# Low parts of weight tiles: a negated copy by ScalarE and an adding DMA in place of a subtraction by POOL

## The chip, the core and the metric

The kernel runs on one core of a Trainium2 chip. The core has five instruction streams that work side by side and wait for one another through semaphores: TensorE (PE, matrix products), VectorE (DVE), ScalarE (ACT), GpSimd (POOL) and SyncE (SP, which here only issues DMAs). Sixteen DMA engines move data between HBM and the on-chip memory (SBUF). Each stream is worked through strictly in the order in which it was written.

The metric is the time of one execution on the device, in microseconds (us); lower is better.

## The reference

One layer of a bidirectional hybrid encoder, in float32, for 1024 tokens of width 1024:

```python
h = _rms_norm(x, g_mix_pre[l])
proj = h @ w_in[l]
...
attn_o = _window_attention(aq, ak, av, attn_sink[l])
dn_o = _gated_deltanet(dqkv, dgate, dalpha, dbeta, conv_w[l], a_log[l], dt_bias[l], g_dn_out[l])
mix = jnp.concatenate([attn_o, dn_o], axis=-1) @ w_out[l]
x = x + _rms_norm(mix, g_mix_post[l])
c = _memory_cross_attention(_rms_norm(x, g_cross_pre[l]), _rms_norm(mem, g_mem[l]), w_cq[l], w_ckv[l], w_co[l])
x = x + _rms_norm(c, g_cross_post[l])
f = _swiglu(_rms_norm(x, g_ffn_pre[l]), w_gate_up[l], w_down[l])
x = x + _rms_norm(f, g_ffn_post[l])
```

What matters here is that all weight matrices pass once through TensorE, and that the products must come out close to float32.

## The kernel before, in words

**High and low parts.** The kernel gives TensorE its operands in a rounded float32 type (fp32r). To keep the accuracy, each operand is split into a high part (the value rounded to fp32r) and a low part (value minus high part, again as fp32r), and a product is made of three: high by high, high by low, low by high. The helper `split(hi, lo, src, scale, eng)` makes the two parts: ScalarE copies `src` into `hi` (line 102), then VectorE or, with `eng=nc.gpsimd`, POOL subtracts (line 103). So every weight tile goes through a chain: DMA load from HBM, ScalarE cast, subtraction, matmuls.

**Weight tiles.** `load_w` (lines 119 to 130) loads a tile of 128 partitions by 1024 floats (512 KB) into `wraw` (line 125) and splits it into `whi` and `wlo`. The pool `wp` has two buffers of each of the three. A new `wraw` can be loaded when the split of the tile two before has read the old one; a new `whi` or `wlo` can be written when the matmuls of the tile two before have read the old one. The loads stand in SP's one queue, between all other DMAs of the kernel, and are given a high priority so that they are placed early.

**Who asks POOL to subtract.** Five callers give `eng=nc.gpsimd`:

- `delta_proj`: 10 of the 12 projections of the DeltaNet part of `w_in`; two matmul halves for each tile (`gemm_b`, line 259).
- `next_keys`: 8 tiles of `w_ckv` (line 902, matmuls on line 906), one in each step of the delta-rule scan, between two window-attention blocks (`ORDER_3`). The scan's steps load `kv` and `pz` (lines 786 and 787) through the same SP queue.
- `cross_q`: 16 tiles of `w_cq` (line 1069), 24 matmuls each, in two rounds of 8; the second round's matmuls stand between those of the first half's cross attention.
- `pair_weights`: 14 tiles of `w_gate_up` for the 7 feed-forward blocks that weren't begun early (line 1240).
- Line 1150: 8 tiles of 128 by 512 of the normed activations (`xraw`), for the feed-forward part.

That makes 48 tiles of 128x1024 and 8 of 128x512. The other splits of weights (60 of 128x1024) are subtracted by VectorE.

**Order.** A scheduler places the instructions of all engines from a timing model of its own when the program is built, so a change in one helper also moves other instructions. `ORDER_1` to `ORDER_3` give the order of the larger steps. Stages, by the span's clock: DeltaNet projections until about 211 us, windows and inverses until about 423, the scan with `next_keys` until about 600, output projection until 689, `cross_q` and cross attention 689 to 803, its output projection and the norm until about 1000, the feed-forward part to the end.

Of the kernel before, what the change touches and what calls it, by code (L numbers as in the profile page):

```python
# [14 lines left out]
ALU = mybir.AluOpType  # L15
# [60 lines left out]
def tile_hybrid_block(  # L76
# [6 lines left out]
    nc = tc.nc  # L83
# [9 lines left out]
    def f32(ap):  # L93
        return ap.bitcast(F32)
# [4 lines left out]
    def split(hi, lo, src, scale=None, eng=None):  # L99

        if scale is None:
            nc.scalar.copy(hi, src)  # L102
            (eng or nc.vector).tensor_tensor(lo, src, f32(hi), ALU.subtract)  # L103
        else:
            nc.scalar.activation(hi, src, AF.Identity, scale=scale)
            nc.vector.scalar_tensor_tensor(lo, src, scale, f32(hi), ALU.mult, ALU.subtract)
# [11 lines left out]
    def load_w(src, k, n, eng=None, after=None):  # L118

        with tc.high_priority(AHEAD):  # L120
            raw = wp.tile([P, k, n], F32, tag="wraw", name="wraw")
            with ExitStack() as order_:
                if after:
                    order_.enter_context(tc.issue_after(after.ins))
                nc.sync.dma_start(raw, src.rearrange("(k p) n -> p k n", p=P))
            hi = wp.tile([P, k, n], F32R, tag="whi", name="whi")
            lo = wp.tile([P, k, n], F32R, tag="wlo", name="wlo")
            split(hi, lo, raw, eng=eng)
        return hi, lo
# [79 lines left out]
    for hf in range(2):  # L209
        hi = hx.tile([P, KT, HALF], F32R, name=f"hhi{hf}")  # L210
        lo = hx.tile([P, KT, HALF], F32R, name=f"hlo{hf}")
        for j in range(4):
            t = 4 * hf + j
            xt = xts[t] if t < 6 else t1.tile([P, D], F32, tag="xt", name="xt", bufs=6)
            if t >= 6:
                nc.sync.dma_start(xt, x[t * P:(t + 1) * P, :])
            junk = t1.tile([P, D], F32, tag="junk", name="junk", bufs=1)
            ss = t1.tile([P, 1], F32, tag="ss", name="ss", bufs=4)
            nc.scalar.activation(junk, xt, AF.Square, accum_out=ss)
            rs = t1.tile([P, 1], F32, tag="rs", name="rs", bufs=4)  # L220
            rstd_of(rs, ss, 1.0 / D, EPS)
            nc.vector.scalar_tensor_tensor(xt, xt, rs, gmix, ALU.mult, ALU.mult)
            for kq in range(2):
                pt = small()
                for k in range(4):
                    c = (4 * kq + k) * P
                    nc.tensor.transpose(pt[:, k * P:(k + 1) * P], xt[:, c:c + P], ident)
                o = slice(4 * kq, 4 * kq + 4), slice(j * P, (j + 1) * P)
                split(hi[:, o[0], o[1]], lo[:, o[0], o[1]], pt.rearrange("p (k t) -> p k t", k=4))
        hT.append((hi, lo))  # L230
        dump(f"hT{hf}", (hi, lo))
# [380 lines left out]
    def window(n, g):  # L612
# [41 lines left out]
        for j in range(nb):  # L654
            pp = pw.tile([P, 512], F32, tag="pw", name="ptw")
            for hh in range(4):
                nc.tensor.transpose(pp[:, hh * P:(hh + 1) * P], pr[hh][:, j * P:(j + 1) * P], ident)
            ph = tw.tile([P, 512], F32R, tag="ph", name="ph")
            pl = tw.tile([P, 512], F32R, tag="pl", name="pl")
            split(ph, pl, pp)  # L660
            for i, pe_ in enumerate((ph, pl)):
                nc.tensor.matmul(po.rearrange("p h t -> p (h t)"), vhl[:, k0 + j, g].rearrange("p r e -> p (r e)"), pe_,
                                 start=(j == 0 and i == 0), stop=(j == nb - 1 and i == 1))
# [846 lines left out]
```

## Time and profile before

| | us |
|---|---|
| median of 3 runs | 1585.95 |
| lowest and highest | 1582.44, 1587.69 |
| span of the profiled execution (first to last instruction) | 1584.2 |
| busy: ScalarE | 762.6 |
| busy: POOL | 498.5 |

The profiled execution has no time of its own beside its span; the median lies 1.75 us above that span.

How the rows are read. A group of instructions has its line, engine, operation, what it writes and reads (`wlo<-wraw,whi`), the shape, the count, then busy time and mean duration in ns, and after the bar the idle time of the engine just before them with what ended it. A row of the timeline has the start in us, the duration in us, the engine, the line and the operation; in square brackets stands the idle time before it. A row on a tile has the shortest, median and longest duration in ns and the first and last start. Matmuls are pipelined: a row's duration is longer than the distance to the next matmul.

### The profile page before, as it was taken

Reading aid. Unit: us, or ns where it says so; the run is one execution under the profiler, and the core shown is the slowest. Engines: PE = TensorE matmul, PEld = TensorE weight load, DVE = VectorE, ACT = ScalarE, POOL = GpSimd, SP = SyncE. Lnnn points to the kernel's source line nnn. Section 1 sums busy time; section 2 is a strip of 40 time slices with the busy share of each in tenths; the row PEclk is TensorE's granted clock in tenths of the full one; section 3 lists DMA queues with packets and bytes.
Section 4 is the critical chain, followed back from the end, with each engine's and each line's share of the span. In section 5 each row is a group of like instructions: output and inputs, shape, how many; then the busy total and the mean of one; then the engine's idle time right before and its main releaser. Section 6 shows DMA issues by size and latency. Waiting matters only on the chain. (4 is left out here: it accounts for less than half of the span.)

```text
span 1584.2 us, 21184 instructions
## 1 busy us (share of the span) xinstructions
PE 1507.2 (95%) x7514; PEld 1261.1 (80%) x7514; DVE 1058.9 (67%) x1616; ACT 762.6 (48%) x1523; POOL 498.5 (31%) x447
## 2 busy tenths in 40 slices
PE   6999889989899989999999999999999999999997
PEld 5877778878689967788888777788888888888786
DVE  6846887985688865544346449677768654596665
ACT  6566543238766785554335566323232332344532
POOL 2368644233134510243301140433434333100021
PEclk9999999989999999999999999999999999999999
DMA  6134148383998576454222254443335333853354
GB/s 207 41 114 130 44 152 228 113 206 104 305 288 277 185 248 204 147 193 151 67 80 81 79 192 139 131 156 120 124 109 166 100 100 101 296 201 113 107 171 161
DMA packets 252151, 242.97 MB, mean 153 GB/s; under 512 B 33528, under 2 KB 187021, under 8 KB 252045
## 3 DMA queue, kind: packets, MB, share of 16 engines
q1 hardware_dynamic: 252045, 241.62, 48.1%
q8 instruction: 59, 0.97, 0.3%
q14 instruction: 47, 0.39, 0.1%
HBM read 172.07 MB, written 66.88 MB: 151 GB/s over the span
## 5 line engine op out<-in xcount | busy, mean ns | idle before, releaser
L102 ACT CAST whi<-wraw 128x1024 fp32r<-128x1024 f32 x108 | 113.3, 1050 | 162.4 <-PE pmg L1006 34.8
L103 POOL TENSOR_TENSOR wlo<-wraw,whi 128x1024 fp32r<-128x1024 f32 x48 | 120.2, 2504 | 192.8 <-ACT whi L102 174.5
L259 PE MATMUL pg<-hlo,whi 128*128 128x512 f32 x352 | 140.3, 399 | 0.0
L259 PE MATMUL pg<-hhi,whi 128*128 128x512 f32 x352 | 140.2, 399 | 0.0
L259 PE MATMUL pg<-hhi,wlo 128*128 128x512 f32 x352 | 140.0, 398 | 0.0
L103 DVE TENSOR_TENSOR wlo<-wraw,whi 128x1024 fp32r<-128x1024 f32 x60 | 74.6, 1244 | 79.9 <-ACT whi L102 75.7
L1006 PE MATMUL pmg<-whi,b 128*128 128x512 f32 x384 | 118.4, 394 | 2.6 <-ACT whi L102 2.2
L1181 PE MATMUL pA<-s,whi 128*128 128x512 f32 x352 | 109.5, 392 | 1.4 <-ACT m L1198 1.4
L284 DVE SCALAR_TENSOR_TENSOR acc<-cp,cols,acc 128x1024 f32<-128x1024 f32 x48 | 73.9, 1540 | 19.5 <-ACT acc L282 18.9
L1006 PEld LDWEIGHTS pmg<-whi,b 128*128 128x128 f32 x384 | 71.2, 188 | 17.9 <-ACT whi L102 2.7
L1258 POOL TENSOR_TENSOR act<-act,up 128x512 f32<-128x512 f32 x33 | 50.1, 1518 | 89.6 <-DVE up L1257 53.1
L259 PEld LDWEIGHTS pg<-hhi,wlo 128*128 128x128 f32 x352 | 67.3, 191 | 13.2
L259 PEld LDWEIGHTS pg<-hhi,whi 128*128 128x128 f32 x352 | 67.2, 191 | 13.4 <-ACT hhi L102 0.3
L259 PEld LDWEIGHTS pg<-hlo,whi 128*128 128x128 f32 x352 | 67.4, 191 | 13.1
L1371 PE MATMUL pdX<-dhl,whi 128*128 128x512 f32 x264 | 76.1, 390 | 1.5 <-DVE zv L1426 0.7
L1181 PEld LDWEIGHTS pA<-s,whi 128*128 128x128 f32 x352 | 65.3, 188 | 15.2 <-ACT m L1198 2.0
L1401 POOL TENSOR_SCALAR frs<-sq 128x1 f32<-128x1 f32 x8 | 12.0, 1500 | 196.0 <-ACT jk L1390 195.0
L1006 PE MATMUL pmg<-wlo,b 128*128 128x512 f32 x192 | 71.4, 391 | 0.0
L1181 PE MATMUL pA<-s,wlo 128*128 128x512 f32 x176 | 68.7, 392 | 1.6 <-DVE wlo L103 1.6
L102 ACT CAST whi<-araw 128x1024 fp32r<-128x1024 f32 (+1 forms) x36 | 35.3, 982 | 70.8 <-PE pdX L1371 27.6
L1230 POOL TENSOR_TENSOR sr<-wraw 128x512 f32<-128x512 f32 x22 | 29.1, 1324 | 125.2 <-DMA wraw<-in_w_gate_up_dram 124.2
L103 DVE TENSOR_TENSOR wlo<-araw,whi 128x1024 fp32r<-128x1024 f32 (+1 forms) x36 | 40.8, 1133 | 38.3 <-ACT whi L102 38.2
(409 smaller groups left out, 4233.3 us busy)
## 6 DMA issues: line engine op xcount, KB each, us to landing
wraw<-in_w_gate_up_dram SPq DMA_DIRECT2D x52, 512.0 KB, 3.9
kv<-d_kv SPq DMA_DIRECT2D x32, 512.0 KB, 6.7
wraw<-in_w_in_dram SPq DMA_DIRECT2D x22, 512.0 KB, 4.2
b<-in_w_down_dram SPq DMA_DIRECT2D x20, 512.0 KB, 7.1
araw<-d_as SPq DMA_DIRECT2D x20, 512.0 KB, 3.8
d_kv<-kv SPq DMA_DIRECT2D x8, 1024.0 KB, 7.1
pz<-d_pz SPq DMA_DIRECT2D x32, 256.0 KB, 6.0
wraw<-in_w_ckv_dram SPq DMA_DIRECT2D x16, 512.0 KB, 7.2
```

The costliest lines, as they stand in the source:

```text
L102: nc.scalar.copy(hi, src)
L103: (eng or nc.vector).tensor_tensor(lo, src, f32(hi), ALU.subtract)
L259: nc.tensor.matmul(p_, w[:, k, :], ah[a][:, k, :], start=(k == 0 and i == 0), stop=(k == nk - 1 and i == 2))
L284: nc.vector.scalar_tensor_tensor(acc, cp[:, t:t + S], taps[t], acc, ALU.mult, ALU.add)
L1006: nc.tensor.matmul(pp[t], act[a][:, k, tt], w_[:, kk, :], start=(k == 0 and i == 0), stop=(k == KT - 1 and i == 2))
L1181: nc.tensor.matmul(out_, w[a][:, k, :], xx[b_][:, k, :], start=(start and k == 0 and i == 0), stop=(k == HK - 1 and i == 2), skip_group_ch ...
L1230: nc.gpsimd.tensor_tensor(s[0], b_[:, 0:HK], b_[:, HK:], ALU.add)
L1258: nc.gpsimd.tensor_tensor(o_, o_, up, ALU.mult)
L1371: nc.tensor.matmul(banks[t], a[:, k - k0, tt], w, start=(first and k == 0 and i == 0), stop=(k == NB - 1 and i == 2), skip_group_check=not ...
L1401: nc.gpsimd.tensor_scalar(rs, sq[:, 1, t:t + 1], sq[:, 0, t:t + 1], D * EPS, ALU.add, ALU.add)
```

## The change

Where POOL was to subtract, ScalarE now writes minus `src` into `lo` (which rounds it to fp32r, so it is minus the high part), and a DMA that POOL issues adds the raw tile to `lo` in place, in float32. Where VectorE subtracts, nothing changes.

```diff
         if scale is None:
             nc.scalar.copy(hi, src)
-            (eng or nc.vector).tensor_tensor(lo, src, f32(hi), ALU.subtract)
+            if eng is nc.gpsimd:
+                nc.scalar.mul(lo, src, -1.0)
+                nc.gpsimd.dma_start(f32(lo), src, accum_op=ALU.add)
+            else:
+                nc.vector.tensor_tensor(lo, src, f32(hi), ALU.subtract)
```

The lines behind line 103 move down by four (`load_w`'s load is line 129 after, `next_keys`' matmuls line 910).

The scheduler places other instructions anew too. Three places show it.

On PE, in the scan, between the first two matmuls of the first `next_keys` tile (which need only `whi`) and the first one that needs its `wlo`; `pck` is the key product, `psc` the scan, `psw`, `ptw` and `pow` the window attention. Before:

```order
L906 MATMUL pck<-mT_4123,whi 128x256
L906 MATMUL pck<-mT_4124,whi 128x256
L778 MATMUL psc<-S,kv 128x128 x4
L634 MATMUL psw<-khi,qs 128x384
L634 MATMUL psw<-klo,qs 128x384
L778 MATMUL psc<-S,kv 128x128 x2
L778 MATMUL psc<-kv,pz 128x128
L662 MATMUL pow<-ph,vhl 128x512
L778 MATMUL psc<-kv,pz 128x128 x2
L906 MATMUL pck<-mT_4123,wlo 128x256
```

And after, the last rows ahead of the same matmul:

```order
L782 MATMUL psc<-S,kv 128x128 x4
L638 MATMUL psw<-khi,qs 128x384
L638 MATMUL psw<-klo,qs 128x384
L638 MATMUL psw<-khi,qs 128x384
L638 MATMUL psw<-klo,qs 128x384
L661 MATMUL ptw<-ident,sc 128x128 x8
L910 MATMUL pck<-mT_4133,wlo 128x256
```

Before, 12 matmuls of other work stand between the second `whi` matmul and the first `wlo` one; after, 82. For the second tile it is 16 before and 18 after, for the third none in both.

On SP, in the scan, around the loads of the fourth and the fifth key tile's `wraw` (after, the third one's too); in brackets the semaphores that a row waits for (`Pool` and `DVE` tell that an engine has finished, `DMASW` that a DMA issued by POOL has landed, `DMAHW` one issued by SP). Before:

```order
L786 DMA kv<-d_kv_99 128x1024 [waits DMAHW4_49,PE_49]
L125 DMA wraw<-in_w_ckv_dram 128x8x128 [waits DMAHW5_49,DVE_49]
L786 DMA kv<-d_kv_99 128x1024 [waits DMAHW6_49]
L125 DMA wraw<-in_w_ckv_dram 128x8x128 [waits DMAHW7_49,Pool_49]
L787 DMA pz<-d_pz_102 128x512 [waits DMAHW0_49]
L786 DMA kv<-d_kv_100 128x1024 [waits DMAHW1_49,PE_49]
```

After:

```order
L129 DMA wraw<-in_w_ckv_dram 128x8x128 [waits DMAHW0_49,DVE_49]
L671 DMA d_mix<-ao 64x4x128 [waits DMAHW1_49,DVE_49]
L129 DMA wraw<-in_w_ckv_dram 128x8x128 [waits DMAHW2_49,DMAHW3_49,DMASW3_49,Activation_49]
L627 DMA qr<-d_q 64x4x128 [waits DMAHW7_49,DMAHW6_49,Pool_49]
L627 DMA qr<-d_q 64x4x128 [waits DMAHW4_49]
L129 DMA wraw<-in_w_ckv_dram 128x8x128 [waits DMAHW0_49,DMAHW5_49,DMASW4_49,Activation_49]
L627 DMA qr<-d_q 64x4x128 [waits DMAHW4_49,DMAHW3_49,Pool_49]
L627 DMA qr<-d_q 64x4x128
L913 DMA d_mk<-cv 128x256 [waits Activation_49]
L791 DMA pz<-d_pz_101 128x512 [waits DMAHW1_49,PE_49]
L791 DMA pz<-d_pz_102 128x512 [waits DMAHW2_49]
L790 DMA kv<-d_kv_99 128x1024 [waits PE_49]
```

The load that waited for POOL's subtraction now waits for the landing of POOL's DMA, and two such loads stand ahead of the next scan step's `pz` and `kv`.

On ACT, in the first round of `cross_q`; `b<-pcq` is the high part of the query product, `s<-ptn` the high part of the second half's normed activations. Before:

```order
L102 CAST whi<-wraw 128x1024
L102 CAST b_6998<-pcq 128x512
L105 ACTIVATE s_6924<-ptn,cols 128x512 x2
L102 CAST whi<-wraw 128x1024
L102 CAST b_6998<-pcq 128x512
L105 ACTIVATE s_6924<-ptn,cols 128x512 x2
```

After:

```order
L104 ACTIVATE wlo<-wraw 128x1024
L109 ACTIVATE s_6942<-ptn,cols 128x512 x4
L102 CAST whi<-wraw 128x1024
L104 ACTIVATE wlo<-wraw 128x1024
L102 CAST b_7016<-pcq 128x512
L102 CAST whi<-wraw 128x1024
L104 ACTIVATE wlo<-wraw 128x1024
```

Each cast of a tile is followed at once by the negated copy of the same tile.

## The prediction

> **What bounds the kernel now.** I read the page first, then the view of the waits, then the tiles that POOL subtracts.
>
> ```profile
> span 1584.2 us, 21184 instructions
> PE 1507.2 (95%) x7514; PEld 1261.1 (80%) x7514; DVE 1058.9 (67%) x1616; ACT 762.6 (48%) x1523; POOL 498.5 (31%) x447
> PE 37%; DVE 2%; DMA 1%; ACT 1%; issue 0%; SPq 0%; POOL 0%; DVEq 0%; POOLq 0%; ACTq 0%
> ```
>
> TensorE is busy in 95% of the span, and the chain that ended last, as far as it could be followed, is nearly all PE, with POOL at 0%. So freeing POOL is worth nothing by itself; the question is whether a low part comes later than TensorE wants it. The next rows are the two groups that the change touches, and three rows of the waits (total us, times, longest us).
>
> ```profile
> L102 ACT CAST whi<-wraw 128x1024 fp32r<-128x1024 f32 x108 | 113.3, 1050 | 162.4 <-PE pmg L1006 34.8
> L103 POOL TENSOR_TENSOR wlo<-wraw,whi 128x1024 fp32r<-128x1024 f32 x48 | 120.2, 2504 | 192.8 <-ACT whi L102 174.5
> ...
> PE ps L227 <- DVE xt L222: 13.6, 5, 8.0
> PE ps L451 <- POOL gm L450: 2.8, 3, 1.5
> SPq L125 <- POOL wlo L103: 149.8, 23, 22.3
> ```
>
> 48 subtractions of 2.5 us each; PE's longest entry is 13.6 us and no row of it names a POOL `wlo`: every one is done in time today. SP's queue, though, stood 23 times before a load because POOL hadn't yet read the buffer.
>
> **What the change does to one tile.** Before: cast, 0.08 us, subtraction, ready. After: cast, negated copy on ScalarE, then X, the time from POOL's issue to the landing of the adding DMA. A ScalarE pass over 128x1024 with a factor takes 1.15 us:
>
> ```profile
> L1026 ACT ACTIVATE xr<-z,pr 128x1024 f32<-128x1024 f32 x16 | 18.2, 1149 | 5.2 <-POOL pr L160 5.2
> ```
>
> The usual subtraction takes 2.4 us (rows below), so the low part comes L = 1.15 + X - 2.4 = X - 1.25 us later. The kernel has no adding DMA and none issued by POOL, so X is bounded by other transfers (KB each, median us to landing):
>
> ```profile
> wraw<-in_w_ckv_dram SPq DMA_DIRECT2D x16, 512.0 KB, 7.2
> wraw<-in_w_cq_dram SPq DMA_DIRECT2D x16, 512.0 KB, 3.5
> rot<-sn SPq DMA_DIRECT2D x40, 64.0 KB, 2.3
> mkr<-d_mk SPq DMA_DIRECT2D x1, 1024.0 KB, 9.3
> ```
>
> Low end: 2.3 us, the SBUF to SBUF row, eight times smaller. High end: 9.3 us for 1 MB plus 2.4 us, if POOL needs as long to write the transfer's description as to subtract: 11.7. I take the row nearest in size and stage, 3.5 us, add 1.4 us because the add must read a second 512 KB ((3.5 - 2.3) us for 448 KB), and 1.1 us, about half of those 2.4, for POOL: **X = 6.0, L = 4.75**. In the scan the same 512 KB takes 7.2 us, 3.7 more: X = 9.7, L = 8.45.
>
> The Trainium skill, page "DMA: Bandwidth & Descriptors", section "Anatomy of one DMA — SWDGE (gpsimd) path", fits such a transfer at 2.0 us plus bytes over 436e3, an estimate of 3.2 us for 512 KB; a second read of that size would make it 4.4. No run shows either here; the second rival says what that X gives.
>
> **The scan (`next_keys`, 8 tiles).** The first three tiles: POOL's row, then the first matmul that reads that `wlo`; last, the stage's windows row (us, busy of PE, PEld, DVE, ACT, POOL, clock, DMA share, GB/s).
>
> ```profile
> 423.94 2.38 POOL L103 TENSOR_TENSOR wlo<-wraw,whi 128x1024 fp32r<-128x1024 f32 x1 [4.23 <-ACT whi L102]
> 427.01 0.36 PE L906 MATMUL pck<-mT,wlo 128*128 128x256 f32 x1
> ...
> 445.66 2.38 POOL L103 TENSOR_TENSOR wlo<-wraw,whi 128x1024 fp32r<-128x1024 f32 x1 [1.23 <-ACT whi L102]
> 450.67 0.36 PE L906 MATMUL pck<-mT,wlo 128*128 128x256 f32 x1
> 459.43 3.67 POOL L103 TENSOR_TENSOR wlo<-wraw,whi 128x1024 fp32r<-128x1024 f32 x1 [7.71 <-ACT whi L102]
> 463.15 0.39 PE L906 MATMUL pck<-mT,wlo 128*128 128x256 f32 x1
> ...
> 423.00:552.00 129.00, 124.52 (x975) 118.94 (x974) 105.86 (x283) 88.46 (x238) 55.90 (x56) 0.99 0.83 263
> ```
>
> Slacks: 427.01 - 426.32 = 0.7 us, 450.67 - 448.04 = 2.6, 463.15 - 463.10 = 0.05. The new order puts 82 matmuls instead of 12 in front of the first; at 129/975 = 0.13 us each the 70 more are worth 9.3 us and cover its L. The second lacks 8.45 - 2.6 = 5.8, the third 8.4; a wait at the second also gives the third time, so together I count the longer, **8.4 us**. Behind them on SP: two `wraw` loads now wait for landings and stand ahead of the next step's `pz` and `kv`, so these go out up to 8.45 us later; as they are fetched a step ahead I count half, **4 us**. And the DMA engines are taken at 0.83 already: 8 tiles that read 1 MB each are 8 MB, at 263 GB/s 32 us of such traffic, or 0.83 x 32/129 = 0.2 of the stage. That leaves hardly any room (0 to 6 us); I count **2**. Scan: 14.
>
> **`cross_q` (16 tiles).** The second half of one tile, the start of the next, and when `wlo` is read first and last in each round:
>
> ```profile
> 708.32 2.41 POOL L103 TENSOR_TENSOR wlo<-wraw,whi 128x1024 fp32r<-128x1024 f32 x1
> 710.99 0.39 PE L259 MATMUL pcq<-b,wlo 128*128 128x512 f32 x1
> ...
> 711.67 0.39 PE L259 MATMUL pcq<-b,wlo 128*128 128x512 f32 x1
> 712.55 1.05 ACT L102 CAST whi<-wraw 128x1024 fp32r<-128x1024 f32 x1 [2.77 <-PE pcq L259]
> 713.38 0.40 PE L259 MATMUL pcq<-b,wlo 128*128 128x512 f32 x1
> 713.68 2.41 POOL L103 TENSOR_TENSOR wlo<-wraw,whi 128x1024 fp32r<-128x1024 f32 x1 [2.95 <-ACT whi L102]
> ...
> L259 PE MATMUL pcq<-b,wlo x64: 389/389/477, 695.3 to 743.9; 128*128 128x512 f32 x64
> L259 PE MATMUL pcq<-s,wlo x64: 387/389/481, 745.4 to 802.6; 128*128 128x512 f32 x64
> ```
>
> Two buffers make a loop: the cast at 712.55 starts when the matmuls of two tiles earlier have ended ("<-PE pcq"). Three matmuls take 711.67 - 710.99 = 0.68 us, a tile's 24 take 5.4, or 5.0 from the first that reads `wlo`. The loop over two tiles is now 1.05 + 0.08 + 1.15 + 0.08 + X + 5.0 = 7.36 + X; at X = 6, 6.7 us per tile. The first round runs at (745.4 - 695.3)/8 = 6.26 per tile, the second at 57.2/7.9 = 7.2. So 0.44 x 8 = 3.5 us in the first, nothing in the second. At the start the slack is smaller than L (713.38 - 710.73 = 2.65 for the tile shown) and I add 1.5: **5 us**. The loop decides from X = 5.2 on.
>
> **The other tiles.** The tightest of `delta_proj`, the tightest of the feed-forward part, and the eight small ones with the first feed-forward product:
>
> ```profile
> 121.74 3.37 POOL L103 TENSOR_TENSOR wlo<-wraw,whi 128x1024 fp32r<-128x1024 f32 x1
> 130.72 0.39 PE L259 MATMUL pg<-hhi,wlo 128*128 128x512 f32 x1
> ...
> 1004.17 2.40 POOL L103 TENSOR_TENSOR wlo<-wraw,whi 128x1024 fp32r<-128x1024 f32 x1 [4.90 <-ACT whi L102]
> 1010.40 0.39 PE L1181 MATMUL pA<-s,wlo 128*128 128x512 f32 x1
> ...
> L103 POOL TENSOR_TENSOR s<-xraw,s x8: 1288/1292/1297, 906.0 to 921.0; 128x512 fp32r<-128x512 f32 x8
> L1181 PEld LDWEIGHTS pA<-s,wlo x176: 186/188/188, 934.2 to 1358.0; 128*128 128x128 f32 x176
> ```
>
> Slacks of 5.6 us (enough for 4.75), 3.8 (0.95 short) and 934.2 - 922.3 = 12 (enough): **1 us**. The cover is the prefetch by one tile; gone, each tile would cost its L.
>
> **Engines.** ScalarE gets 48 x 1.15 + 8 x about 0.6 = 60 us, beside 820 us in which it is idle; even in the scan it has 129 - 88 = 40 us free for 9.2 more. I count **1** (0 to 9, the scan's share if nothing hides it). What POOL gives back shows in three rows:
>
> ```profile
> 695.60 1.28 DVE L1020 SCALAR_TENSOR_TENSOR z<-z,prs,xr 128x1024 f32<-128x1024 f32 x1
> 695.92 3.21 POOL L103 TENSOR_TENSOR wlo<-wraw,whi 128x1024 fp32r<-128x1024 f32 x1
> 697.45 2.77 DVE L1020 SCALAR_TENSOR_TENSOR z<-z,prs,xr 128x1024 f32<-128x1024 f32 x1 [0.58 <-DMA xr<-in_x_dram]
> ```
>
> The same VectorE operation takes 1.28 us alone and 2.77 beside POOL's subtraction. Half of 48 such meetings would be 24 x 1.5 = 36 us of VectorE, which has 525 idle; I count **-2** on the path (0 to -10).
>
> **Sum:** 14 + 5 + 1 + 1 - 2 = +19 us on the span of 1584.2, so 1603; the median of the runs lies 1.75 above that span: **1605 us**.
>
> **Rivals.**
> *The landing is slow.* If X lies between 9 and 11.7, the loop costs (8.2 - 6.26) x 8 + (8.2 - 7.2) x 8 = 23 to 45 us, the scan about 19 to 25, the other tiles 7 to 17: after the last two engine terms 48 to 86 in all, 1634 to 1672. For it: the DMA share of 0.83 in the scan, 0.63 in the first round of `cross_q`. Against it: 3.5 us for a plain load of this size there.
> *The landing is hidden.* At X = 4.4 everywhere L is 3.15: the loop of `cross_q` makes 5.9 us per tile and waits for nothing, the scan loses 3.1 + 1.5, and with +1 and -2 the sum is +4: 1590, no change that can be told (a difference within 0.3%, 4.8 us, can't be told here). Against it: the 7.2 us in the scan.
> *VectorE is relieved, and it gets faster.* One mechanism: POOL no longer reads SBUF beside VectorE, on the DeltaNet and feed-forward stretches, where VectorE feeds PE. It decides if more than 10 of those 36 us lie on PE's path while X stays at 4.4 or below: 1586 + 4 + 2 - 12 = 1580. Against it: PE's list names no wait of more than 13.6 us in total.
> The Trainium skill, page "SBUF — State Buffer", section "Who interferes with whom", says that a VectorE instruction with two SBUF inputs contends with a GpSimd one that reads SBUF; the 2.77 against 1.28 us agree, and by it the subtraction's going is all gain for VectorE.
>
> **Chances.** Forecast 0.58 (with small deviations), slow landing 0.20, hidden 0.15, relieved 0.07. Faster by over 0.3%: 0.07; within: 0.15; slower: 0.78. The range reaches from the hidden case's lower edge, 1584, into the slow landing, 1645; outside lie most of the relief (0.07) and the far part of the slow landing (0.12).
>
> **What would show it.** After, POOL's DMA row should land in 6 us in `cross_q` and near 10 in the scan; PE should name the landing DMA as what it waits for, some 8 us in the scan's second and third tile and some 5 in `cross_q`; SP should stand before `wraw` for the landing. Landings of 4 us, or a scan whose PE doesn't wait, would make the forecast wrong downwards; over 9, or waits in `delta_proj` and the feed-forward part, upwards.

## The result, and the profile after

| | us |
|---|---|
| after, median of 4 runs (lowest, highest) | 1629.82 (1628.24, 1634.8) |
| before, on the same chip, median of 4 runs | 1584.64 (1582.44, 1587.69) |
| ratio, 95% interval | 1.0285, 1.0269 to 1.03 |
| span of the profiled execution after (before) | 1628.7 (1584.2) |

Slower by 45 us, where 19 were forecast. (Of the ten executions of e4 below, one took 3034.84 us where the others took 1580.8 to 1586.1; it counts as slow and is left out of the ratio.) First the page of after: the span, the busy times, the chain that ended last, the group of POOL's DMA issues and the time from such an issue to the landing.

```profile
span 1628.7 us, 21330 instructions
PE 1524.8 (94%) x7514; PEld 1271.6 (78%) x7514; DVE 1030.8 (63%) x1616; ACT 806.8 (50%) x1577; POOL 409.5 (25%) x447
PE 58%; DMA 10%; ACT 6%; DVE 6%; issue 2%; POOL 2%; SPq 1%; DVEq 0%; POOLq 0%; ACTq 0%
L105 POOL DMA_DIRECT2D wlo<-wraw x48 | 42.4, 883 | 233.5 <-ACT wlo L104 191.2
wlo<-wraw POOLq DMA_DIRECT2D x48, 512.0 KB, 4.6
```

Each engine that the change relieves is relieved: POOL by 89 us, VectorE by 28. Neither bounds the kernel: in the chain that ended last POOL has 2% and VectorE 6%. DMA, 1% of the chain before, now has 10%. PE is busy 17.6 us longer with the same 7514 matmuls, so some of them ran slower, and the remaining 27 of the 44.5 us are idle. In the view of the waits after (us in all, times, longest) PE's first entry is that of before, 13.6 us there; the other two are new:

```profile
PE ps L231 <- DVE xt L226: 13.8, 5, 8.4
...
PE pcq L263 <- DMA wlo<-wraw: 8.7, 4, 4.8
...
SPq L129 <- DMA wlo<-wraw: 196.8, 31, 13.9
```

Where the time went is read from the windows. I cut both spans at the same events: the start of the first `psc` (scan), the end of the last `pcv` (value product for the cross attention), the end of the first half of the output projection's `pmg`, the end of the last `pco` (output of the cross attention), the start of the first `pA` (first feed-forward product) and the end of the last `pE` (last of these products). The feed-forward products begin at 934 us before, earlier than the list of stages above has it. Columns: us, then busy us and instructions of PE, PEld, DVE, ACT and POOL, the clock granted to TensorE, DMA share, GB/s. Before:

```profile
407.30:598.00 190.70, 178.65 (x1242) 162.04 (x1243) 148.00 (x368) 136.94 (x346) 62.98 (x64) 0.97 0.81 262
598.00:695.00 97.00, 92.74 (x421) 75.89 (x420) 49.32 (x52) 48.77 (x76) 14.67 (x22) 1.00 0.47 162
695.00:903.60 208.60, 206.01 (x1038) 172.38 (x1038) 97.56 (x149) 97.79 (x190) 52.58 (x43) 1.00 0.34 111
903.60:934.00 30.40, 30.40 (x150) 25.23 (x148) 11.17 (x13) 18.40 (x37) 12.49 (x12) 1.00 0.40 129
934.00:1364.00 430.00, 425.52 (x1882) 349.41 (x1881) 300.09 (x372) 153.28 (x244) 153.03 (x103) 1.00 0.41 134
```

After:

```profile
407.70:612.30 204.60, 183.14 (x1245) 164.59 (x1245) 147.94 (x369) 144.40 (x354) 50.26 (x64) 0.96 0.87 264
612.30:712.50 100.20, 94.55 (x417) 77.83 (x418) 49.23 (x50) 49.73 (x77) 13.15 (x22) 0.97 0.46 155
712.50:938.50 226.00, 211.80 (x1039) 175.47 (x1038) 92.25 (x149) 111.63 (x205) 29.25 (x43) 0.97 0.52 140
938.50:972.40 33.90, 30.54 (x149) 25.00 (x147) 9.47 (x12) 22.02 (x45) 8.10 (x10) 0.99 0.73 171
972.40:1407.60 435.20, 429.52 (x1881) 352.84 (x1882) 293.83 (x373) 164.80 (x258) 127.56 (x105) 0.99 0.50 150
```

Each row gives two things beside its length: length minus PE's busy time is PE's idle time, and (1 - clock) times length is what a reduced clock took at most, since a low clock costs nothing while PE waits. In the third row idle goes from 208.6 - 206.0 = 2.6 to 226.0 - 211.8 = 14.2 us, and the clock from 1.00 to 0.97, 0.03 x 226 = 6.8 us; PE's busy time, with one matmul more, grows by 211.8 - 206.0 = 5.8. By stage:

| stage | longer by | PE idle, before, after | lost to half clock at most, before, after |
|---|---|---|---|
| scan with the key tiles | 14.0 | 12.0, 21.4 | 5.8, 8.9 |
| output projection, first half | 3.2 | 4.3, 5.7 | 0, 3.4 |
| `cross_q` and cross attention | 17.3 | 2.6, 14.2 | 0, 6.8 |
| up to the first feed-forward product | 3.5 | 0, 3.4 | 0, 0.4 |
| feed-forward | 5.2 | 4.5, 5.7 | 0, 4.8 |

The stretch ahead of the scan and the end add 1.3. The last column is half the length of the single half-clock segments of the trace, summed.

The first of the waits in `cross_q`, in the timeline of after (start, duration, in brackets the idle time and its releaser):

```profile
708.29 0.94 POOL L105 DMA_DIRECT2D wlo<-wraw  x1 [36.18 <-ACT wlo L104]
...
713.45 0.73 PE L263 MATMUL pcq<-b,whi 128*128 128x512 f32 x2 [0.46 <-ACT whi L102]
...
718.96 0.80 PE L263 MATMUL pcq<-b,wlo 128*128 128x512 f32 x1 [4.78 <-DMA wlo<-wraw]
```

And the windows around it and behind it:

```profile
715.50:722.50 7.00, 3.54 (x8) 2.82 (x9) 3.17 (x3) 4.73 (x10) 3.78 (x9) 0.51 1.05 303
722.50:730.00 7.50, 7.50 (x35) 6.18 (x34) 0.69 (x1) 5.61 (x7) 1.01 (x3) 1.00 0.94 323
```

The low part was ordered at 708.29 and is there at 718.9: 10.6 us, and PE waits 4.8 for it. This is the first tile of the round. Then comes the second price: for 7 us the clock stands at 0.51; PE still waits in 3.5 of them, and in the rest a matmul of this shape lasts 0.80 us where it usually lasts 0.39. The same pair, waits and half a clock behind them, stands at the last two tiles of the round, first in the timeline, then in a window:

```profile
764.77 0.73 PE L263 MATMUL pcq<-b,whi 128*128 128x512 f32 x2 [1.98 <-ACT whi L102]
767.66 0.80 PE L263 MATMUL pcq<-b,wlo 128*128 128x512 f32 x1 [2.15 <-DMA wlo<-wraw]
```

```profile
766.00:774.00 8.00, 6.34 (x16) 5.05 (x17) 1.89 (x3) 1.12 (x3) 0.83 (x1) 0.57 1.00 307
```

### The profile page after: what moved, and what is told of

The parts are those of the page before. It is cut to its first block, busy times and chain, and to the rows that moved or that the text cites. A ratio compares the mean times of both kernels' runs of the same rounds, so it can differ in the third digit from the quotient of the medians.

```text
span 1628.7 us, 21330 instructions
## 1 busy us (share of the span) xinstructions
PE 1524.8 (94%) x7514; PEld 1271.6 (78%) x7514; DVE 1030.8 (63%) x1616; ACT 806.8 (50%) x1577; POOL 409.5 (25%) x447
## 4 chain that ended last, share of the span: by engine, by line
PE 58%; DMA 10%; ACT 6%; DVE 6%; issue 2%; POOL 2%; SPq 1%; DVEq 0%; POOLq 0%; ACTq 0%
PE pmg L1010 8%; PE pE L1185 7%; PE pD L1185 7%; PE pA L1185 6%; PE pdX L1375 5%; PE pcq L263 5%; PE pdA L1375 4%; PE pB L1185 4%; PE psc L782 3%; PE pdD L1375 2%; DMA wlo<-wraw 2%; DMA wraw<-in_w_gate_up_dram 1%; PE pco L1117 1%; PE pg L263 1%; PE pcs L1091 1%
## 5 line engine op out<-in xcount | busy, mean ns | idle before, releaser
L105 POOL DMA_DIRECT2D wlo<-wraw x48 | 42.4, 883 | 233.5 <-ACT wlo L104 191.2
L288 DVE SCALAR_TENSOR_TENSOR acc<-cp,cols,acc 128x1024 f32<-128x1024 f32 x48 | 69.7, 1456 | 38.6 <-ACT acc L286 38.0
L263 PEld LDWEIGHTS pg<-hhi,wlo 128*128 128x128 f32 x352 | 67.8, 193 | 13.9 <-DMA wlo<-wraw 0.3
L1405 POOL TENSOR_SCALAR frs<-sq 128x1 f32<-128x1 f32 x8 | 11.9, 1496 | 196.0 <-ACT jk L1394 195.1
```

The lines of the kernel that those rows point to most:

```text
L105: nc.gpsimd.dma_start(f32(lo), src, accum_op=ALU.add)
L263: nc.tensor.matmul(p_, w[:, k, :], ah[a][:, k, :], start=(k == 0 and i == 0), stop=(k == nk - 1 and i == 2))
L288: nc.vector.scalar_tensor_tensor(acc, cp[:, t:t + S], taps[t], acc, ALU.mult, ALU.add)
```

## The experiments

Theory A, formed from these traces: the landing time counts, where SP's loads share the DMA engines, and half clock makes each wait dearer. Rival B: every tile has its price, by ScalarE's added pass and by the order that follows from it. In all kernels with a single site, `split` takes the new path for that site and POOL subtracts at the others. All ratios are to the kernel before, run on the same chip; stages are cut as above.

A stage's time comes from one execution, so its scatter has to be known. Ten of these kernels (e1, e3, e4, e6 to e10, e14, e15) have PE, VectorE and POOL in the scan in the order of before, and their scan differs from that of before by -1.6 to +2.6 us; half clock takes 1.7 to 7.2 us there. The `cross_q` stage takes 208.6 us in every kernel whose `cross_q` tiles are subtracted as before, and the stretch up to the first `pA` 30.3 or 30.4 in all whose small tiles are (but e6). So a difference of some 4 us in the scan can be scatter; in the other two it can't.

### One site at a time

```diff
-            if eng is nc.gpsimd:
+            if eng == "dma":
                 nc.scalar.mul(lo, src, -1.0)
                 nc.gpsimd.dma_start(f32(lo), src, accum_op=ALU.add)
             else:
-                nc.vector.tensor_tensor(lo, src, f32(hi), ALU.subtract)
+                (eng or nc.vector).tensor_tensor(lo, src, f32(hi), ALU.subtract)
...
-            whi, wlo = load_w(w_cq[:, ct * P:(ct + 1) * P], KT, P, nc.gpsimd)
+            whi, wlo = load_w(w_cq[:, ct * P:(ct + 1) * P], KT, P, "dma")
```

The other three differ in the callers that say `"dma"`.

> Only the 16 tiles of cross_q get the negated copy and the adding DMA; the other 40 stay with POOL's subtraction. Theory A (the landing of the adding DMA is too late for the loop over two buffers, and the DMA is slow where SP's other transfers are in flight): +17 us against before, nearly all between the first and last product of cross_q, with landings of 8 to 10 us beside other loads and 4.5 alone. Rival B (each moved tile costs about the same, by ScalarE's extra pass and the new order: 45 us over 56 tiles): +13 us, spread over the kernel.

> Only the 8 key tiles of the scan get the adding DMA. Theory A: +14 us, all in the scan. Rival B: 8 of 56 tiles, +6 us.

> Only the 14 feed-forward tiles and the 8 small activation tiles get the adding DMA. Theory A: these have 4 us of slack or more, so within +-3 us; the 8 us that the changed kernel loses behind cross_q come with its other tiles. Rival B: 22 of 56 tiles, +18 us.

> Only the 10 DeltaNet tiles get the adding DMA. Theory A: slack of 5.6 us and more against a delay of some 3 us, so 0, or a gain of up to 3 us because POOL no longer subtracts beside VectorE. Rival B: 10 of 56 tiles, +8 us.

| run | ratio, interval | where |
|---|---|---|
| e1, `cross_q` | 1.0102, 1.0078 to 1.0126 | its stage +14.9 (idle 2.6 to 12.1, half clock 0 to 6.8) |
| e2, key tiles | 1.0099, 1.0068 to 1.013 | scan +16.1, output projection +2.9 |
| e3, feed-forward and small tiles | 1.0051, 1.0032 to 1.0071 | +4.2 up to the first `pA`, +5.7 behind it |
| e4, DeltaNet tiles | 0.9977, 0.9964 to 0.9991 | -3.4 before the scan, -1.4 in it |

e1 and e2 speak for A, though 14.9 lies close to B's 13 too. e3 misses the ±3 that A gave it. e4 is a small gain. The stages add up: 14.9 + 16.1 + 2.9 + 4.2 + 5.7 = 43.8, and the change has 43.2 in the same five. The ratios add up less well, to 1.023 against 1.0285: e4's gain doesn't show in the change, and e2's stages come from the slowest of its four executions (1607.43 us, median 1604.48).

### The same without a DMA

```diff
-                nc.gpsimd.dma_start(f32(lo), src, accum_op=ALU.add)
+                nc.gpsimd.tensor_tensor(lo, f32(lo), src, ALU.add)
```

> All 56 tiles: ScalarE writes minus the raw tile as in the change, but POOL adds the raw tile with a tensor_tensor of about 2.4 us where the change issues a DMA. (The high part is not subtracted here either, as in no place of the change the kernel's ScalarE output would allow it otherwise: ScalarE writes minus the high part's source, so this run has the same ScalarE work, the same kind of order and no DMA.) Theory A (the landing: the low part is late because the transfer lands 4.5 to 10 us after its issue, in the first round of cross_q and the scan late enough that PE waits): the low part is only the ScalarE pass, 1.15 us, later than before, under the slacks of most tiles; +0 to +6 us, ratio 1.000 to 1.004, PE idle in the cross_q stage at most 5 us. Rival B (a cost of every tile: the ScalarE pass and the order that follows from it): +25 to +45 us, ratio above 1.015, PE idle in the cross_q stage about 12 us as with the DMA.

(What the bracket in that text means: `lo` holds minus the high part, so POOL's addition gives the same low part.)

Ratio 1.0077, 1.0049 to 1.0106; +14 us, between the two. By stage it is plain: `cross_q` +0.9, up to the first `pA` 0.0, scan +1.4; instead DeltaNet's part +4.9 (half clock up by 4.4 at most) and feed-forward +6.2. So ScalarE's pass, with the order that the scheduler writes for it, isn't what costs the three places where the change loses (1.4 in the scan lies within the scatter); the DMA is, by its landing or by the order written for it. Why this variant loses in two other stages wasn't followed up.

### Which tiles of `cross_q`, and why

A third pair of buffers for the high and low parts of `cross_q` (e6), the first round's 8 tiles only (e7), and these 8 with a DMA that copies without adding (e10) or moves 8 KB instead of 512 (e14). These two leave out the subtraction, e14 in all but the 8 KB; only their times count:

```diff
# e6
+            whi, wlo = load_w(w_cq[:, ct * P:(ct + 1) * P], KT, P, "dma", pl=tx, b=3)
# e7
+            whi, wlo = load_w(w_cq[:, ct * P:(ct + 1) * P], KT, P, ("dma" if hf == 0 else nc.gpsimd))
# e10, beside e7's
+                nc.gpsimd.dma_start(f32(lo), src)
# e14, beside e7's
+                nc.gpsimd.dma_start(f32(lo)[:, 0, 0:16], src[:, 0, 0:16], accum_op=ALU.add)
```

> As e1_cross_only (the 16 tiles of cross_q by the adding DMA, the others subtracted by POOL), but high and low part of cross_q's tiles have three buffers of their own. Theory A (two buffers close a loop of about 7.4 us plus the landing time over two tiles; with three it runs over three tiles, (7.4 + 8)/3 = 5.1 us per tile, under the 6.26 that the matmuls take): the loss of +16 to +18 falls to +2 to +7, ratio 1.001 to 1.005; PE idle in the stage from 12 back to 3 to 6 us, no segment of half clock there or one. Landing times stay as they were, 4.5 to 10 us. Rival B (a cost of every tile, however many buffers there are): +14 to +18, ratio about 1.010.

> As e1_cross_only, but only the 8 tiles of the first round of cross_q go by the adding DMA; the second round's 8 are subtracted by POOL again. Theory A (the loss arises where the transfers meet SP's loads and stores, in the first round; in the second they land in 4.5 to 5 us, which the loop has room for): +13 to +18 us, ratio 1.008 to 1.012, as with both rounds. Rival B (a price per tile): half, +7 to +9, ratio about 1.005.

> As e7_cross_first (8 tiles of the first round of cross_q), but the DMA copies the raw tile over the low part and adds nothing; the subtraction is left out for these 8 tiles. Theory A (the adding transfer holds the DMA engines about twice as long per byte as a plain one, and that is what makes it land late between SP's transfers): a lone one lands in 3 to 3.5 us where the adding one takes 4.5, the median in this round falls from 8 to 5 or 6, and the loss of +17 to +4 to +9 us, ratio 1.0025 to 1.006. Rival B (it is late because it queues behind what SP has issued, whatever it does itself): median 7 to 8 us and +14 to +17, ratio 1.009 to 1.011.

> As e7_cross_first (8 tiles of the first round of cross_q), but the adding DMA covers 16 of each partition's 1024 elements only; in the others the low part is minus the raw tile, the subtraction is left out there. ScalarE's pass, POOL's issue and the wait for a landing stay; the order in the stage changes with it. Theory A (the loss of 17.1 us in this stage is the time that transfers of 512 KB take to land among SP's): landings of 2 to 4 us, the loop takes 7.4 + 3 = 10.4 us for two tiles, under the matmuls' 12.5; stage 0 to +4, ratio 1.000 to 1.003. Rival O (order, the ScalarE pass, the issue): stage +8 or more.

**e6 told nothing of the loop.** 1.0373 (1.0349 to 1.0397), worse than any. With the third buffers the scheduler drew `cross_q` together, and 174 of the 1038 matmuls moved behind the last `pco`. The transposes that were now without cover waited instead, as these groups of its PE (last: idle time before them) show:

```profile
L1107 PE MATMUL pct<-ident,cpr 128*128 128x128 f32 x64 | 11.1, 305 | 11.0 <-DVE cpr L1101 5.7 <-ACT cpr L1098 5.0 <-ACT whi L102 0.3
L979 PE MATMUL ptn<-ident,xr 128*128 128x128 f32 x40 | 9.7, 401 | 11.4 <-ACT xr L1030 8.6 <-DVE s L110 2.8
```

**e7 puts the loss into the first round:** 1.0108 (1.0092 to 1.0124), stage +17.1, as with both rounds. e10 and e14 follow the landing down. The rows on `wlo`, e7 first, then e10 and e14: POOL's issues, PE's wait for them (us, times), time to landing.

```profile
L105 POOL DMA_DIRECT2D wlo<-wraw x8: 859/862/1072, 691.2 to 749.7; - x8
...
  PE pcq L263: 9.3, 4
...
DMA to landing us min/median/max: 4.5/8.0/10.9
```

```profile
L105 POOL DMA_DIRECT2D wlo<-wraw x8: 530/530/783, 693.0 to 745.9; - x8
...
  PE pcq L263: 5.1, 2
...
DMA to landing us min/median/max: 2.9/4.8/8.9
```

```profile
L105 POOL DMA_DIRECT2D wlo<-wraw x8: 859/862/1072, 688.8 to 736.6; - x8
...
  PE pcq L263: 1.5, 2
...
DMA to landing us min/median/max: 2.0/4.0/6.6
```

| run | median landing | stage | PE idle | half clock at most | ratio, interval |
|---|---|---|---|---|---|
| e7, adds 512 KB | 8.0 | +17.1 | 14.2 | 6.8 | 1.0108, 1.0092 to 1.0124 |
| e10, copies 512 KB | 4.8 | +10.2 | 8.3 | 5.1 | 1.0079, 1.0062 to 1.0096 |
| e14, adds 8 KB | 4.0 | +2.3 | 4.3 | 0 | 1.0026, 1.0014 to 1.0038 |

e7 and e10 have the same order on every engine, so their difference, 6.9 us, is the transfer's alone; e10's 12.5 us in all (0.0079 of 1585) lie above A's 4 to 9 and below B's 14 to 17: two landings still take 8.7 and 8.9, and PE waits 5.1 us for them. With e14, ScalarE's pass, the issue and a wait for a landing are all still there, and 15 of the 17 us are gone. That excludes B here and settles the place for A, with one thing open: the scheduler wrote e14 in another order than e7, so beyond the 6.9 us the shorter landing and the order that goes with it can't be told apart.

### The small tiles

```diff
-        split(x1h[:, k, :], x1l[:, k, :], raw[:, k, :], eng=nc.gpsimd)
+        split(x1h[:, k, :], x1l[:, k, :], raw[:, k, :], eng="dma")
# e15, beside that
+                nc.gpsimd.dma_start(f32(lo)[:, 0:16], src[:, 0:16], accum_op=ALU.add)
```

> Only the 8 small activation tiles (128x512, ahead of the first feed-forward product) go by the adding DMA, all others are subtracted by POOL. Theory A (the last of these small transfers land about 8 us after issue, just before the feed-forward product wants them, so its start moves by some 4 us, and a segment of half clock behind that idle time doubles it): +4 to +8 us, ratio 1.0025 to 1.005, the most of it before the first pA matmul. Rival C (the 14 feed-forward tiles cost it, in the stage where the half-clock segments lie): 0 to +3 us, ratio below 1.002.

> As e8_x1l_only (the 8 small activation tiles), but the adding DMA covers 16 of each partition's 512 elements only; the subtraction is left out in the others. Theory A (the eight transfers hold the DMA engines while SP's load of the next gate and up weights goes; that load lands late, ScalarE's cast of it stands ahead of the emptying of the PSUM banks which the first feed-forward product needs): that load lands in 6 to 8 us again instead of 10.9, the stretch up to the first pA loses 0 to 1 instead of 4.1 us, ratio 1.000 to 1.002. Rival O (ScalarE's eight added passes, 0.65 us each, and the order): it still loses 3 to 4, ratio 1.004 to 1.007.

e8: 1.0066 (1.0049 to 1.0083), as much as e3 lost within the intervals and more than the +4 to +8 us expected: +4.1 up to the first `pA`, +4.3 behind it (e3: +4.2, +5.7), so the 14 feed-forward tiles have a small part at most. e15, which leaves out the subtraction in all but 8 KB of each tile: 1.0014 (1.0 to 1.0027), 0.0 up to the first `pA`; up to there every engine has e8's order, so the size of the transfers alone makes the difference. The chain is in the timeline. Before, SP's load of the gate and up weights, ScalarE's cast of it, and the emptying of the PSUM banks behind the cast:

```profile
923.45 8.79 SPq L125 DMA_DIRECT2D wraw<-in_w_gate_up_dram  x3
929.54 1.05 ACT L102 CAST whi<-wraw 128x1024 fp32r<-128x1024 f32 x1 [5.44 <-DMA wraw<-in_w_gate_up_dram]
930.76 0.60 ACT L1009 ACTIVATE z<-pmg 128x512 f32<-128x512 f32 x1 [0.16 <-PE pmg L1006]
```

With the eight small DMAs (e8), and PE's first `pA`; then the window behind it:

```profile
925.14 14.08 SPq L129 DMA_DIRECT2D wraw<-in_w_gate_up_dram  x3
936.53 1.04 ACT L102 CAST whi<-wraw 128x1024 fp32r<-128x1024 f32 x1 [10.69 <-DMA wraw<-in_w_gate_up_dram]
937.48 0.59 ACT L1013 ACTIVATE z<-pmg 128x512 f32<-128x512 f32 x1
939.49 1.22 PE L1185 MATMUL pA<-s,whi 128*128 128x512 f32 x2 [3.90 <-DVE z L1014]
```

```profile
939.50:947.00 7.50, 7.28 (x25) 5.59 (x26) 7.50 (x8) 4.13 (x8) 7.07 (x9) 0.80 0.78 269
```

Nobody waits for a small tile. But the load issued at 925 is there only 11 us later (before: 6); ScalarE stands at the cast of it, and queued behind that cast are the copies that empty the PSUM banks, for which the first `pA` waits 3.9 us; then half clock (0.80 over the next 7.5 us). This isn't the way that e8's expectation had it, by the small tiles themselves. Behind it, at 992 us, `pA` waits once more, 2.5 us for ScalarE's `m`, where before the longest such wait is 0.7; what makes that one longer is open. In the view of the DMA issues the load has a median of 5.7 us before, 10.9 in e8, 6.2 in e15.

### The scan

The raw tiles of the keys loaded from POOL's queue (e11), the copy in place of the adding (e12), 8 KB (e13), and the kernel before with an 8 KB copy of the raw tile to a scratch tile behind POOL's subtraction, so that only the release of `wraw` waits for a landing (e16). e12 and e13 leave out the subtraction, e13 in all but 8 KB of each tile:

```diff
# e11
-                nc.sync.dma_start(raw, src.rearrange("(k p) n -> p k n", p=P))
+                (q or nc.sync).dma_start(raw, src.rearrange("(k p) n -> p k n", p=P))
...
+        whi, wlo = load_w(w_ckv[:, ct * P:(ct + 1) * P], KT, P, "dma", q=nc.gpsimd)
# e12 and e13, beside e2's: the lines of e10 and e14
# e16: POOL subtracts
             split(hi, lo, raw, eng=eng)
+            if scr:
+                nc.gpsimd.dma_start(scr.tile([P, 16], F32, tag="scr", name="scr", bufs=2), raw[:, 0, 0:16])
```

> As e2_keys_only (the 8 key tiles of the scan by the adding DMA), but the raw tiles of these 8 are loaded from POOL's queue, so that SP never stands before a load until the adding DMA that reads the buffer has landed. Theory S (SP's standing, 25 us in 6 times, makes the loads of pz, kv and qr behind it late, and with them the window attention and the scan's steps): SP's entry for that landing goes, qr lands in about 4 us again, the scan stage falls from +16 to 0 to +6, ratio 1.001 to 1.005. Rival C (the transfers themselves take the DMA engines' time from pz, kv and qr): scan stage +10 to +16, ratio 1.008 to 1.011, qr still at 8 to 9 us. A third way would be POOL's queue standing instead and with it the window attention's POOL work: then PE waits for POOL es.

> As e2_keys_only (8 key tiles of the scan), but the DMA copies the raw tile over the low part and adds nothing; the subtraction is left out for these 8 tiles. Every engine's instructions stand in the same order as in e2_keys_only. Theory C (the adding transfers take the DMA engines' time and land late among pz, kv and qr; a copy holds the engines half as long, as in e10_cross_copy, where the stage's loss fell from 17.1 to 10.2): scan stage from +16 to +6 to +10, median landing from 7.8 to about 6. Rival O (the order that the scheduler wrote for the scan costs it, whatever the transfer takes): scan stage stays at +14 to +16.

> As e2_keys_only, but the adding DMA covers 16 of each partition's 1024 elements only, so the low part is minus the raw tile in the others; the subtraction is left out there. The order in the scan changes with it, but ScalarE's pass, POOL's DMA issue and the wait for a landing stay. Theory C (transfer time and landing): the landing takes 2 to 3 us, SP stands for it less than 10 us in all, scan stage -1 to +4. Rival O (ScalarE's pass, the issue and the rewritten order cost it): scan stage +10 or more.

> The kernel before (POOL subtracts all tiles), with one more thing at the 8 key tiles: after the subtraction POOL issues a DMA that copies 16 elements of each partition of the raw tile to a scratch tile that nobody reads. So the low part comes as before, but the raw buffer is free only when a landing has come, 2 to 6 us later, and SP's next load stands for it. Theory S (of e13_keys_tiny's +9.7 in the scan the wait of the raw buffer for a landing is the most): scan stage +5 to +10. Rival L (it is the low part's own lateness, by which the scheduler writes another order): scan stage 0 to +3, ratio 1.000 to 1.002.

| run | scan stage | PE idle (before 12.0) | half clock at most (before 5.8) | ratio, interval |
|---|---|---|---|---|
| e2, adds 512 KB | +16.1 | 23.1 | 8.2 | 1.0099, 1.0068 to 1.013 |
| e11, loads from POOL's queue | +13.9 | 20.9 | 12.2 | 1.0116, 1.0098 to 1.0134 |
| e12, copies 512 KB | +12.7 | 19.3 | 12.0 | 1.0097, 1.008 to 1.0114 |
| e13, adds 8 KB | +9.7 | 17.4 | 10.1 | 1.0085, 1.007 to 1.01 |
| e16, POOL subtracts, `wraw` waits | -3.5 | 11.9 | 2.2 | 0.9962, 0.9947 to 0.9977 |

What PE waits for in the scan of the change itself, the longest entries:

```profile
PE psw L638 <- DVE pl L107: 4.8, 2, 4.3
PE pow L666 <- ACT ph L102: 3.9, 5, 2.2
PE psw L638 <- DVE m L640: 2.9, 4, 0.9
PE psc L782 <- DMA pz<-d_pz: 2.3, 1, 2.3
```

No low part of a key is among them; the window attention is late. SP's queue alone is not why: in e11 it stands for the landing of a key's DMA 3.9 us (e2: 24.9), `qr` lands in 4.8 us again (e2: 8.9), and the stage still loses 13.9. But POOL's queue stood in its stead, 14.9 us in 4 times. That the raw tile is released late needn't cost: e16 has that and loses nothing, less than either side expected. It doesn't clear SP, though, which stands for these landings there once, and in e13 seven times (SP's waits in the scan, e13, then e16):

```profile
SPq L129 <- DMA wlo<-wraw: 29.0, 7, 6.1
```

```profile
SPq L129 <- DMA scr<-wraw: 7.2, 1, 7.2
```

The transfer's size shows no sure part. With e2's order kept on every engine, e12 halves the DMA queue's share (queue of POOL's transfers in the scan's window: packets, MB, share of 16 engines; e2, then e12):

```profile
q0 software_dynamic: 1152, 4.19, 10.9%
```

```profile
q0 software_dynamic: 1152, 4.19, 5.7%
```

The median landing stays at 7.5 us (e2: 7.8), though, the stage gains 3.4 us, within the scatter, and the ratios of the two are the same within their intervals. With 8 KB (e13) 9.7 us remain, where rival O expected 10 or more. There the low part comes 1.15 + 4.3 - 2.4 = 3 us later than by POOL (4.3 is e13's median landing); with e5's 1.15 us later the stage loses 1.4. So in the scan most of the price comes with a low part that is some 3 us late and depends little on the transfer's size (1.0099 for 512 KB, 1.0085 for 8). Whether it is the lateness itself, the order that the scheduler writes for it, or a queue that stands for landings (SP's, or in e11 POOL's) can't be told here: that stays open.

### The tiles that cost nothing

> Only the 10 tiles of delta_proj and the 14 of the feed-forward part go by the adding DMA; those of the scan, of cross_q and the 8 small ones are subtracted by POOL as before. Theory A (the transfer costs only where SP's loads share the DMA engines with it and something waits for them; these 24 tiles have slack, and VectorE is relieved of POOL beside it): the -3.6 us of the 10 tiles alone is kept and the 14 add 0 to -2: -3 to -6 us, ratio 0.996 to 0.998, faster than the kernel before. Rival B (half of what the 14 and the 8 cost together belongs to the 14): -3.6 + 4, so 0 to +2 us, ratio about 1.000.

The edits are those of e4 and of the 14 feed-forward tiles together. Ratio 1.0017, 1.0001 to 1.0032: e4's gain did not come along (before the scan -1.3 in place of -3.4), and the feed-forward stage gave +1.9. That is near rival B's number, though its reason, half of e3's loss for the 14 tiles, doesn't hold, as e8 shows; the 14 cost 1 to 2 us (5.7 - 4.3 between e3 and e8, 1.9 here). e4 at 0.9977 and e16 at 0.9962 are the two kernels faster than before; in e16 a copy that nobody reads changes the order, and the scan takes 3.5 us less. I read gains of this size as luck of the order, not as the relief of an engine.

## Why the prediction was wrong in size

Direction, range and several terms held; the sum of +19 was 26 short. By stage the 44.5 us of the spans are 17.3 in `cross_q`, 14.0 in the scan, 8.7 from the last `pco` to the last `pE`, 3.2 in the output projection and 1.3 elsewhere.

- **`cross_q`, +5 forecast, +17.3 measured: the term that failed.** What was mis-sized is X: the prediction put one number, 6.0, for all 16 tiles. Second-round tiles land in 4.5 to 5.1 us and cost nothing, as forecast; the first round's, among `xr`, `z` and `gpost`, take 4.5 to 10.6, on average 7.65. The loop is there (the casts of the later tiles wait for `PE pcq`), but PE's waits come from single late landings: 5.2 us at the first tile, where the step counted 1.5 for the start (a landing of 10.6; 4.8 for the low part, 0.5 for the cast), 4.1 at the last two tiles (a landing of 10.3) and 1.7 between. For the tiles behind the first that makes 5.9, where the step's formula with 7.65 gives ((7.36 + 7.65)/2 - 6.26) x 8 = 10.0. That the formula and the 1.5 together make 11.5, and PE's idle time rose by 11.6, is luck. The 0.63 DMA share of that round stood in the prediction, but only as an argument of a rival. **Half clock** was in no term; PE's busy time in the stage grew by 5.8.
- **Scan, +14 forecast, +14.0 measured, by another road.** 8.4 us were to be direct waits of PE for landings: there are none. 4 us were to come from SP's standing: e11 speaks against SP alone, and no run settles it. The 2 us for the crowded DMA engines aren't shown either: halving the engines' time won 3.4 us in one execution and nothing in the ratios (e12). The sum was right by chance, and what costs the 14 us stays open. The +3.2 in the output projection behind it was not foreseen; it is 2.0 to 3.6 in each kernel with key tiles by DMA and -0.7 to +2.8 in the others, so a part of it may be scatter.
- **The other tiles, +1 forecast, +8.7 measured.** The slack of 12 us for the small tiles was right: no matmul waits for them. What the step left out is that their transfers make another load late, 10.9 us in place of 5.7 (e8), and that the cast of that load stands ahead of the emptying of PSUM on ScalarE. That gives the 3.5 us up to the first `pA`; of the 5.2 behind it, 4.0 are PE at a lower clock (429.5 - 425.5 busy), after that wait and another of 3.2 us for ScalarE's `m`. Crowding was counted in the scan only. The 14 large tiles were all but covered (1 to 2 us), and those of `delta_proj` too (landings of 4.5 to 4.8 us).
- **ScalarE, +1.** About right where the change loses: e5 has the same pass and costs 0.9, 0.0 and 1.4 us at the three places.
- **VectorE, -2.** Its busy time fell by 28 of the 36 us reckoned. On the path e4 shows at most -3.6 (0.0023 of 1586), and e9 not even that. One reading behind the term was wrong: the VectorE row of 1.28 us isn't alone, it starts at 695.60 and runs to 696.88, beside POOL's subtraction from 695.92 on. Only the row that began while the subtraction was running, at 697.45, took 2.77, so not every meeting costs 1.5 us.
- **X.** Forecast 6.0 in `cross_q` (4.5 to 10.6 measured), 9.7 in the scan (median 7.5 for the eight key tiles), nothing said of quiet stretches (4.5). The rival of a slow landing, 9 to 11.7 with 1634 to 1672, is what four of the sixteen tiles in the scan and the first round met (9.9 to 10.6), and the time came out just below its lower edge.

The Trainium skill, page "DMA: Bandwidth & Descriptors", section "Anatomy of one DMA — SWDGE (gpsimd) path", has a fit from which the prediction worked out an estimate of 3.2 us for 512 KB, and 4.4 with a second read. The quiet landings agree: 2.9 for the copy (e10), 4.5 for the adding. In busy stretches, where the adding took up to 10.9 us (e7), the fit doesn't hold; the section says nothing of traffic on other queues.

## What to carry to other kernels

A DMA that replaces an engine's work pays twice on the DMA side: its own landing is as late as the traffic of its stage makes it, and the loads beside it land later; so look for who stands behind those loads, not only for who reads the new transfer. Reckon a landing for each stage with the transfers in flight there, at its late end, and count a short wait of TensorE with the half clock behind it. And where a scheduler writes the order, a change of one latency moves a stage by several us either way, so small gains must be shown by more than one kernel.

## What was not expected of the hardware

- **Half clock after short waits.** With a wait of 4.8 us the granted clock was 0.51 over 7 us, and after 3.9 us 0.80 over 7.5. Over the whole span PE's busy time with the same matmuls grew by 17.6 us, 0.4 of the loss. The Trainium skill, page "TensorE: Matmul & The Clock Gate", section "Part 1: The HAM clock gate (the "warmup" mystery)", says that TensorE falls to half its clock after an idle window of about 3.4 us. The wait of 3.9 us agrees. In that of 4.8 the clock was down after little more than 1.4 us of it (two windows within the wait, both with PE idle):

```profile
714.20:715.60 1.40, 0.00 (x0) 0.00 (x0) 0.25 (x1) 1.40 (x4) 0.95 (x2) 1.00 1.06 275
715.70:718.90 3.20, 0.00 (x0) 0.00 (x0) 0.94 (x1) 1.30 (x4) 2.27 (x6) 0.50 1.03 325
```

The one at 767 us doesn't agree, with 1.98 and 2.15 us and matmuls between them, and in the output projection of after a single wait of 2.23 us has 3.4 us at half clock behind it (timeline, then window):

```profile
674.28 2.19 PE L1010 MATMUL pmg<-whi,b 128*128 128x512 f32 x5 [2.23 <-ACT whi L102]
```

```profile
674.70:678.10 3.40, 3.40 (x10) 2.66 (x9) 1.92 (x2) 0.47 (x1) 0.00 (x0) 0.50 0.35 116
```

Here the measurement decides: waits of little over 2 us can be enough.
- **An adding DMA holds the DMA engines twice as long as a copy of the same bytes:** 10.9% against 5.7% of the scan's window for 4.19 MB (e2, e12), and its issue keeps POOL 0.86 us against 0.53 (e7, e10).
- **A small transfer can be late too in a busy stage:** 8 KB took 2.0 to 6.6 us in `cross_q` (median 4.0, 512 KB 8.0) and 2.1 to 6.0 in the scan (4.3, 7.8).
